# Four model layers on one core: rounding the weights four jobs ahead instead of two

## The chip, the cores and the metric

The kernel runs on one core of a Trainium2 chip in a single launch. TensorE (PE in the profile) multiplies matrices, VectorE (DVE), ScalarE (ACT) and GpSimd (POOL) do elementwise work, and SyncE (SP) issues the transfers of the weights from the chip's memory. Each engine runs its own instructions in the order in which they were written and waits on semaphores for the others. The metric is device time in microseconds (us). The kernel before has a median of 2395.09 us in three runs (2394.77 to 2395.71).

## The reference

256 tokens of 2048 features pass through four residual layers and a last norm, all in float32. Cut to the structure:

```
x = x + cat(chunked_attention(q,k,v) * silu(z_a), glu(gelu(s5(u))) * silu(z_b)) @ w_out   # E1
x = x + forgetting_attention(q,k,v, log_f) * silu(z) @ w_out                              # O1
x = rmsnorm(x)
x = x + cat(hgrn2(q,f,v) * silu(g), nsa(q, six K/V, gates) * silu(g)) @ w_out             # E2
x = x + rglru(conv4(xb)) * silu(g) @ w_out                                                # O2
out = rmsnorm(x)          # q, k, v, u, z, ... are column groups of rmsnorm(x) @ w_in
```

`s5` is a complex state space model of 64 groups, `nsa` sparse attention over 16 heads with compressed keys and values (an MLP on blocks of 32 tokens) and three gates for each head, `rglru` a gated linear recurrence.

## The kernel before, in words

**The stream of weights.** Nearly all of the time goes into the projections. The weights are cut into some 740 *jobs*. A job is two blocks of 128 rows by 512 columns, 512 KB, held as one raw tile of 128x1024. SP loads it (`issue`, the DMA at L281). A float32 product is made of three products of rounded parts: ACT copies the raw tile to a rounded tile `hi` (helper L214), DVE writes the rest `lo` = raw − hi (helper L165), and PE multiplies hi by both parts of the activations and lo by their rounded part (L420). In the W orientation a job is 24 matmuls of 128x256, in the X orientation 12 of 128x512. The activations are split in the same way, once for each group of four feature blocks, into two 4 KB *slots* from a pool of 35 (`Act.split`).

**The loop** (`Kern.run`, L267) emits job by job. At the start of job i, `ahead(i)` calls `prep` for the jobs behind it as long as their width, counted in pieces of 512 columns, stays within `LOOK`; a job counts two. `prep` emits the ACT copy, the DVE subtraction and, if the job's activations are ready, their split. Then come the raw tiles' transfers (`issue(done + RAW)`), the matmuls of job i, and one step of the background. `RAW` is the number of raw tiles, `HL` that of hi and of lo tiles each. So in before the hi and lo of job i+2 are emitted ahead of job i's matmuls, and they need the tiles of job i−2.

**Eleven jobs aren't split**: the forget gate's columns in O1 (one job), the compression weights of E2 (eight, "cmp", in four pairs, L1836 and L219) and its gates (two, "gate", right behind the last pair). PE reads their raw tile itself, so the tile comes free only when their matmuls are done.

**The background** is everything else: attention, S5, HGRN2, NSA, recurrences, norms. Each is a generator, queued in `lane`s. `bg_step` lets each live one do a step after each job, held back by an estimate of how busy DVE, ACT and POOL are, by free PSUM banks and by free slots. If a job's activations are not there yet, the loop forces background steps until they are (`while not all(a.ready ...)`). So the order on every engine comes out of this planning when the program is built, and it changes when `prep` runs earlier: splits and slots are then taken sooner.

**Two places matter below.** At E1's end the gated unit (GLU) multiplies y, the S5's output; y is made block by block, eight blocks, and the second half of the GLU's rows (its first job is number 116) needs the last block (number 7). At E2's end the projection out multiplies the NSA heads' outputs; job 550 needs the last four heads.

Of the kernel before, what the change touches and what calls it, by code (L numbers as in the profile page):

```python
# [11 lines left out]
OP = mybir.AluOpType  # L12
# [14 lines left out]
class Act:  # L27
    """256 columns of tokens for `n` blocks of 128 features, as two float32r parts."""
# [42 lines left out]
class Kern:  # L71
    RAW, HL, LOOK, JK = 5, 4, 4, 2
# [123 lines left out]
    def smax(self, out, a, b, acc):  # L196
        """out = -(a + b); acc = its least, the negative of the greatest of a + b"""
        self._ew('D', self._n(out))
        self.nc.vector.tensor_tensor_reduce(out=out, in0=a, in1=b, op0=OP.add, op1=OP.min,  # L199
                                            scale=-1.0, scalar=3.0e38, accum_out=acc)  # L200
# [26 lines left out]
    def lane(self, gens, width=1, prio=0, name=""):  # L227
        """a queue of (condition, generator maker), `width` of them at a time"""
# [5 lines left out]
    def bg_step(self, force=False):  # L234
# [9 lines left out]
        for L in list(self.lanes):  # L244
            while len(L['live']) < L['width'] and L['q'] and L['q'][0][0]():
                L['live'].append(L['q'].pop(0)[1]())
            for g in list(L['live']):
                if not force and max(self.busy.values()) > self.clock + self.SLACK and L['prio'] > 0:
                    return moved
                # not before what it waits for on another engine is done  # L250
# [3 lines left out]
                try:  # L254
                    r = next(g)
# [11 lines left out]
    def run(self):  # L267
        jobs = self.jobs
        units = []
# [15 lines left out]
        def prep(i):  # L285
            if i >= len(jobs):
                return
            j = jobs[i]
            raw = units[j['u']][1][:, :j['n']]
# [23 lines left out]
        def ahead(i):  # L313
            """the splits of the jobs after job i, as far as LOOK goes"""
# [12 lines left out]
        for i, j in enumerate(jobs):  # L327
            ahead(i)
            # a raw tile is free again once all of it is read
# [29 lines left out]
    def group(self, name, src, acts, orient, post, units, ready=None, bg=False):  # L359
        """one group of 512 columns: `units` is the list of (DRAM AP, kt count)"""  # L360
# [66 lines left out]
def kmap(acts):  # L427
    """k-tile index -> (Act, block in it)"""
    out = []
    for a in acts:  # L430
        out += [(a, i) for i in range(a.n)]
    return out


class Norm:
    """1 / sqrt(mean of squares + eps) for each token, the same on all partitions"""
# [7 lines left out]
    def add(self, src, cols=None):  # L444
        """src: a slot with four blocks of features"""
# [15 lines left out]
    def mean(self, out, extra=None):  # L461
        """generator: out = mean of squares (+ eps), then 1/sqrt"""
# [25 lines left out]
def rsqrt(K, y, v, t):  # L488
    """y = 1 / sqrt(v): a first value by exp(-ln(v) / 2), then a step of Newton"""
# [11 lines left out]
def together(*gens):  # L501
    """the operations of several chains by turns"""
# [9 lines left out]
def steps(n, gen):  # L512
    """n operations at a time"""
# [34 lines left out]
def sincos_ops(K, s, c, x, a, b, d):  # L548
    """sin and cos of x; a, b, d: scratch"""
# [31 lines left out]
    # n mod 4 in -2..2, then a turn by n quarters  # L581
# [10 lines left out]
    K.tt('D', z, z, n, OP.mult)                      # sine of the turn  # L592
    yield
    K.ts('D', r, r, -1.0, 1.0, OP.mult, OP.add)      # cosine of the turn
# [15 lines left out]
def evac_scaled(K, ps, rs, out=None):  # L610
    """a feature-major group times a row of tokens' factors"""
# [13 lines left out]
def evac_silu(K, ps, rs_half, done):  # L625
    """x times sigmoid(x): with h = x / 2 it is (tanh(h) + 1) h"""
# [12 lines left out]
def token_scales(K, rs, out):  # L639
    """generator: factors by token on partitions"""  # L640
# [8 lines left out]
def soft_rows(K, p, nm, sm, cols):  # L649
    """p holds -(s); exp(s - max) with its sums. cols: [(first, end)]"""  # L650
# [4 lines left out]
class E1:  # L655
    """relative-position attention in chunks beside an S5 state space model"""
# [41 lines left out]
    def build(self):  # L698
# [8 lines left out]
        def post_u(i):  # L707
            def f(ps):
                if not self.norm_ok or K.slots.free < 3:
                    return 'wait'  # L710
                # even tokens before odd ones
# [5 lines left out]
                def stack():  # L717
                    """both tokens of a pair on the partitions, for two tiles of states at a time"""
# [66 lines left out]
        def load_bias(hg):  # L785
            def gen():
                [s] = yield from K.gslots(1)
                K.nc.sync.dma_start(s, D['e1_bias'][hg])
                # keys of the chunk after the query's own are out of reach
# [138 lines left out]
        # the first half of y before the second  # L928
# [6 lines left out]
    def s5(self):  # L935
# [30 lines left out]
        def powers():  # L966
            """cosine and sine of 2, 4, .. 128 angles"""
# [9 lines left out]
        def coefs():  # L977
            """A, and the factor of B: (A - 1) / lambda"""
# [20 lines left out]
        def pre():  # L999
# [9 lines left out]
            def times(out, v, re, im, tm):  # L1009
                """a complex number for each state times its coefficients"""  # L1010
# [16 lines left out]
            # cosines and sines of 0, 2, .. 30 times each state's angle  # L1027
# [20 lines left out]
            # y takes the real part: the imaginary parts of C with their sign turned  # L1048
# [7 lines left out]
        def fill(e, pad, src, b):  # L1056
            """block b's coefficients, zero outside of each state's own channels"""
# [11 lines left out]
        def block(b):  # L1069
            def gen():  # L1070
# [7 lines left out]
                # the projections in, the channels of each tile's pairs of tokens on their own rows  # L1078
# [4 lines left out]
                # cosines and sines of 0, 2, .. 254 times each state's angle  # L1083
# [21 lines left out]
                # two tokens a step  # L1105
# [42 lines left out]
                # the even tokens' own inputs: C B  # L1148
# [28 lines left out]
                # gelu by tanh, twice its value  # L1177
# [22 lines left out]
        def yz(i):  # L1200
            def gen():
                # y times silu(z), a quarter of (2 y) (2 silu): y_t is 2 y; sigmoid's half is still to come
# [13 lines left out]
class Layer:  # L1216
    """what the layers share: the norm at their start and the sum with the residual at their end"""
# [15 lines left out]
    def begin(self):  # L1233
        """called when the projection out of the layer before starts"""
# [24 lines left out]
    def take(self, g, ps, xr):  # L1259
        """four blocks of the sum: the residual, and this layer's input"""  # L1260
# [13 lines left out]
def out_proj(K, D, wname, n, acts, xr, nxt, tag):  # L1274
    """xr: list of the residual's slots (filled by the time of use)"""
# [12 lines left out]
def attend(K, S_mm, bias, pv, out, left, done, heads=2):  # L1288
    """generator: two heads at a time, queries on partitions. S_mm(bank, e) emits the scores of head e
    (queries 0..127 with keys 0..127 in columns 0..127, queries 128..255 in columns 128..383)"""  # L1290
# [39 lines left out]
def log1p_ops(K, out, z, s, w, d):  # L1330
    """log(1 + z) for z in 0..1, by the series of atanh(z / (2 + z))"""
# [1074 lines left out]
```

## Time and profile before

| what | value |
|---|---|
| median of the runs | 2395.09 us |
| profiled execution, span | 2394.8 us |
| weight and other data read | 396.00 MB |
| PE busy | 98% of the span |
| DVE busy | 66% |
| ACT busy | 48% |
| DMA engines busy, mean | 51% (queue 1 50.7%) |

The profiled execution's own time is known only as its span; what lies around it is the 0.3 us between span and median. PE's share says that the kernel is a stream of matmuls with few gaps. How the gaps end is told by the waits of PE (which engine and line released it, the total, how often, the longest), by the timeline, and by the granted clock (PEclk, as a share of full speed).

### The profile page before, as it was taken

The page shows a single profiled execution, that of the slowest core. Times are in us where ns is not written, and L with a number is a line of the kernel's source. Part 1 is how long each engine was busy: PE and PEld are TensorE (multiplying, and loading weights), DVE is VectorE, ACT ScalarE, POOL GpSimd, SP SyncE. Part 2 cuts the span into 40 slices and gives each one's busy share as a digit, 9 for nine tenths or more (in the row PEclk, how much of TensorE's full clock was granted, in tenths as well). Part 3 has the DMA queues.
Part 4 walks back from the last instruction along what each step waited for, and adds up shares of the span by engine and source line. Part 5 has one row for each costly group of instructions (what it writes and reads, how often), then busy time and mean ns, then how long its engine had stood idle before and what let it go on. Part 6 is the DMA issues. An engine that isn't in the chain of part 4 may idle for free.

```text
span 2394.8 us, 47663 instructions
## 1 busy us (share of the span) xinstructions
PE 2336.9 (98%) x19906; PEld 2253.3 (94%) x19906; DVE 1585.9 (66%) x2409; ACT 1152.5 (48%) x1662; POOL 386.8 (16%) x320
## 2 busy tenths in 40 slices
PE   7999999999999999999999999999999999999997
PEld 7989998999999999989999999899999999999997
DVE  7978878675554545676758574566667446777764
ACT  5354454444444344543445443455555434666643
POOL 1111211010000000123324253101110000111210
PEclk9999999999999999999999999999999999999999
DMA  6544454555545555554544454554444555555453
GB/s 225 191 152 149 142 177 153 175 186 164 193 160 175 174 170 185 169 177 156 170 160 159 162 165 159 192 178 142 142 142 143 195 183 180 165 175 168 161 196 111
DMA packets 116167, 402.23 MB, mean 168 GB/s; under 512 B 14832, under 2 KB 17776, under 8 KB 115952
## 3 DMA queue, kind: packets, MB, share of 16 engines
q1 hardware_dynamic: 115952, 399.19, 50.7%
q8 instruction: 156, 2.56, 0.4%
q14 instruction: 59, 0.48, 0.1%
HBM read 396.00 MB, written 2.10 MB: 166 GB/s over the span
## 4 chain that ended last, share of the span: by engine, by line
PE 84%; DVE 8%; POOL 2%; issue 2%; ACT 2%; DMA 1%; DVEq 0%; SPq 0%; ACTq 0%; POOLq 0%
PE mm L420 75%; PE b L219 6%; DVE lo L165 3%; DVE s L165 2%; POOL s L165 2%; DVE s L194 1%; DVE s L176 1%; PE b L224 1%; PE b L420 1%; ACT s L214 1%; ACT hi L214 1%; DMA raw<-in_e_in 1%; PE b L1836 0%; DVE s L170 0%; DMA s<-in_e_bias 0%
## 5 line engine op out<-in xcount | busy, mean ns | idle before, releaser
L420 PE MATMUL mm<-s,hi 128*128 128x256 f32 x9984 | 1830.5, 285 | 10.4 <-ACT s L214 7.6
L420 PEld LDWEIGHTS mm<-s,hi 128*128 128x128 f32 x9984 | 1563.9, 193 | 18.3 <-ACT s L214 8.0
L420 PE MATMUL mm<-s,lo 128*128 128x256 f32 x4992 | 1418.6, 284 | 24.5 <-DVE lo L165 24.4
L165 DVE TENSOR_TENSOR lo<-raw,hi 128x1024 fp32r<-128x1024 f32 x730 | 934.0, 1294 | 622.2 <-ACT hi L214 620.4
L214 ACT ACTIVATE hi<-raw 128x1024 fp32r<-128x1024 f32 x730 | 756.9, 1054 | 646.1 <-PE mm L420 557.5
L420 PEld LDWEIGHTS mm<-s,lo 128*128 128x128 f32 x4992 | 960.8, 192 | 28.9 <-DVE lo L165 28.8
L165 POOL TENSOR_TENSOR s<-s,s 128x512 f32<-128x512 f32 (+1 forms) x128 | 273.9, 2154 | 1411.4 <-ACT s L214 586.9
L214 ACT ACTIVATE s<-s 128x1024 f32<-128x1024 f32 (+6 forms) x188 | 132.9, 713 | 263.3 <-DVE s L165 137.2
L420 PE MATMUL mm<-hi,s 128*128 128x512 f32 x768 | 244.6, 394 | 0.0
L219 PE MATMUL b<-s,s 128*32 128x32 f32 (+8 forms) x3008 | 175.0, 244 | 4.8 <-POOL s L186 2.1
L420 PEld LDWEIGHTS mm<-hi,s 128*128 128x128 f32 x768 | 145.0, 189 | 30.8 <-ACT s L214 0.3
L219 PEld LDWEIGHTS b<-s,s 128*32 128x32 f32 (+2 forms) x2976 | 148.3, 135 | 23.4 <-POOL s L186 2.5
L420 PE MATMUL mm<-lo,s 128*128 128x512 f32 x384 | 150.5, 392 | 1.6 <-DVE lo L165 1.6
L214 ACT ACTIVATE s<-b 128x384 f32<-128x384 f32 (+6 forms) x135 | 57.2, 462 | 134.9 <-PE b L219 92.7
L165 DVE TENSOR_TENSOR s<-s,s 128x512 f32<-128x512 f32 (+8 forms) x134 | 85.8, 666 | 45.7 <-ACT s L214 44.5
L420 PEld LDWEIGHTS mm<-lo,s 128*128 128x128 f32 x384 | 72.6, 189 | 16.7 <-DVE lo L165 2.4
L176 DVE SCALAR_TENSOR_TENSOR s<-s,s 128x1024 f32<-128x1024 f32 (+3 forms) x76 | 82.6, 1089 | 3.1 <-ACT s L214 2.2
L214 ACT ACT_TABLE_LOAD x44 | 56.5, 1283 | 16.1 <-DVE s L176 14.7
L204 DVE COPY_PREDICATED s<-hmask,b 32x64 f32<-32x64 int32 (+1 forms) x144 | 36.0, 250 | 30.4 <-PE b L219 26.6
L214 ACT ACTIVATE s<-s,nsam 128x15 f32<-128x15 f32 (+2 forms) x96 | 37.6, 394 | 36.0 <-DVE nsam L199 36.0
L170 POOL TENSOR_SCALAR s<-alibi 128x256 f32<-128x256 f32 x16 | 17.8, 1111 | 212.3 <-PE b L219 174.1
L186 POOL MEMSET s<- 128x512 f32 (+7 forms) x65 | 25.8, 410 | 123.3 <-DMA s<-in_e_bias 59.1
(148 smaller groups left out, 966.6 us busy)
## 6 DMA issues: line engine op xcount, KB each, us to landing
raw<-in_e_in SPq DMA_DIRECT2D x336, 512.0 KB, 4.1
raw<-in_o_in SPq DMA_DIRECT2D x208, 512.0 KB, 4.0
raw<-in_e_out SPq DMA_DIRECT2D x80, 512.0 KB, 4.2
raw<-in_o_out SPq DMA_DIRECT2D x72, 512.0 KB, 4.4
raw<-in_e_outa SPq DMA_DIRECT2D x16, 512.0 KB, 3.6
raw<-in_o_rg SPq DMA_DIRECT2D x10, 512.0 KB, 3.7
raw<-in_e_glu SPq DMA_DIRECT2D x8, 512.0 KB, 3.8
raw<-in_e_cmp SPq DMA_DIRECT2D x8, 512.0 KB, 5.1
```

The source lines that it names most:

```text
L165: self._eng(e).tensor_tensor(out, a, b, op=op)
L170: self._eng(e).tensor_scalar(out, a, s1, None, op0=op0)
L176: self.nc.vector.scalar_tensor_tensor(out, a, s, b, op0=op0, op1=op1)
L186: self._eng(e).memset(out, v)
L194: self.nc.vector.tensor_tensor_scan(out, d0, d1, init, op0=OP.mult, op1=OP.add)
L204: self.nc.vector.copy_predicated(out, mask, a)
L214: self.nc.scalar.activation(out, a, func, scale=scale, **kw)
L219: self.nc.tensor.matmul(out, l, r, start=start, stop=stop, skip_group_check=True, **kw)
L224: self.nc.tensor.transpose(out, a, self.ident[:p, :p])
L420: self.nc.tensor.matmul(out, l, r, start=start, stop=stop, skip_group_check=True)
```

## The change

`LOOK` goes from 4 to 8, so that `prep` runs four jobs ahead instead of two. `HL` goes from 4 to 6 and `RAW` from 5 to 4. `prep` first makes sure that the raw tile of its job has been issued. The program's "dynamic DMA scratch" in the on-chip memory is set to 512 bytes per partition in place of the default of 16384; that pays for the tiles, which take 16 KB more of hi and lo and 4 KB less of raw per partition. All else in the diff is comments taken away, so line numbers behind L289 are one higher after.

```
@@ class Kern
-    RAW, HL, LOOK, JK = 5, 4, 4, 2
+    RAW, HL, LOOK, JK = 4, 6, 8, 2
@@ def prep(i)
             j = jobs[i]
+            issue(j['u'] + 1)
             raw = units[j['u']][1][:, :j['n']]
@@ def kernel
-    nc = bacc.Bacc("TRN2", target_bir_lowering=False, num_devices=1)
+    nc = bacc.Bacc("TRN2", target_bir_lowering=False, num_devices=1, dynamic_dma_scratch_size=512)
```

PE's program has the same instructions in the same order outside of two stretches: E1's jobs 0 to about 120, and E2's jobs 534 to 552. On ACT and DVE the splits stand two jobs earlier against the background everywhere.

**E1's end.** On ACT before, hi_4963 is the rounded weight of job 116, s_4008 the gelu chain of the last S5 block, and s_4866 the split of y's second half, which job 116 multiplies:

```order
L214 ACTIVATE s_4008<-s_4008 128x256
L214 ACTIVATE hi_4802<-raw_4590 128x1024
L214 ACTIVATE s_4008<-s_4008 128x256
L214 ACTIVATE hi_4835<-raw_4635 128x1024
L214 ACTIVATE s_4866<-s_3569 128x1024
L214 ACTIVATE hi_4871<-raw_4677 128x1024
L214 ACTIVATE hi_4901<-raw_4709 128x1024
L214 ACTIVATE hi_4933<-raw_4772 128x1024
L214 ACTIVATE hi_4963<-raw_4806 128x1024
```

On ACT after, job 116's weight is hi_4795; behind it come block 6's gelu (s_4244), block 7's states (s_4969), block 7's gelu (s_4366) and then the split s_5034 of y's second half:

```order
L214 ACTIVATE hi_4795<-raw_4639 128x1024
L214 ACTIVATE hi_4832<-raw_4673 128x1024
L214 ACTIVATE hi_4899<-raw_4713 128x1024
L214 ACTIVATE s_4244<-s_4244 128x256
L214 ACTIVATE hi_4934<-raw_4757 128x1024
L214 ACTIVATE s_4244<-s_4244 128x256
L214 ACTIVATE s_4969<-s_1119 64x8x16 x2
L214 ACTIVATE s_4969<-s_105 64x8x16 x2
L214 ACTIVATE s_4366<-s_825 64x8x16 x2
L214 ACTIVATE hi_4978<-raw_4799 128x1024
L214 ACTIVATE s_4366<-s_4366 128x256 x2
L214 ACTIVATE s_5034<-s_3872 128x1024
```

The split of y stood four weight tiles before the tile of the job that uses it, and now stands five behind it. On PE after, all of block 7 (its 32x32 products, and behind them the rest, which needs copies of these) stands between the job before (mm_4905) and job 116 (mm_4801):

```order
L421 MATMUL mm_4905<-s_3323,lo_4754 128x256
L219 MATMUL b_4985<-s_4969,s_4366 32x32 x8
L219 MATMUL b_4985<-s_862,s_4969 128x128
L219 MATMUL b_4985<-s_4523,s_4969 32x128 x4
L219 MATMUL b_4985<-s_4524,s_4969 32x128 x8
L219 MATMUL b_4985<-s_4523,s_4969 32x128 x4
L219 MATMUL b_4985<-s_4523,s_4969 32x127 x4
L219 MATMUL b_4985<-s_4524,s_4969 32x127 x8
L219 MATMUL b_4985<-s_4523,s_4969 32x127 x4
L421 MATMUL mm_4801<-s_5034,hi_4795 128x256
```

The last S5 block moved to the place just in front of the job that needs it.

**E2's end.** On PE before, b_20348 is the last NSA head's output; the job behind it uses the earlier split s_20286, and the split of the last heads (s_20430) is first used 96 matmul rows further on:

```order
L219 MATMUL b_20348<-s_20102,s_16778 128x128
L219 MATMUL b_20348<-s_20102,s_16947 128x128
L420 MATMUL mm_19902<-s_20286,hi_20282 128x256
L420 MATMUL mm_19902<-s_20287,hi_20282 128x256
L420 MATMUL mm_19902<-s_20286,lo_20283 128x256
```

On PE after, b_20481 is the last head's output and s_20501 the split of the last heads:

```order
L219 MATMUL b_20481<-s_20247,s_16785 128x128
L219 MATMUL b_20481<-s_20247,s_16956 128x128
L421 MATMUL mm_19883<-s_20501,hi_20344 128x256
L421 MATMUL mm_19883<-s_20502,hi_20344 128x256
L421 MATMUL mm_19883<-s_20501,lo_20345 128x256
```

The four jobs that lay between the last head and the job that needs it now lie before that head.

## Rows read from the trace of the kernel before

**Rows 1.** The page: busy us, share of the span and instructions of each engine.
```profile
PE 2336.9 (98%) x19906; PEld 2253.3 (94%) x19906; DVE 1585.9 (66%) x2409; ACT 1152.5 (48%) x1662; POOL 386.8 (16%) x320
```

**Rows 2.** PE's waits, whole span: line, releaser, us in total, times, longest.
```profile
PE mm L420 <- DVE lo L165: 26.0, 21, 2.6
PE mm L420 <- ACT s L214: 7.6, 2, 7.3
PE b L224 <- POOL s L182: 2.2, 1, 2.2
PE b L219 <- POOL s L186: 2.1, 1, 2.1
```

**Rows 3.** PE's waits in 0:120, 360:420, 900:1080 and 2040:2340 us.
```profile
PE mm L420 <- DVE lo L165: 5.9, 3, 2.6
...
PE mm L420 <- DVE lo L165: 3.2, 3, 1.4
...
PE mm L420 <- DVE lo L165: 5.0, 5, 1.1
...
PE mm L420 <- DVE lo L165: 11.9, 10, 2.0
```

**Rows 4.** The chain that ended last: start, us, engine, line, matmuls.
```profile
1831.41 169.91 PE mm L420 x1416
```

**Rows 5.** Timeline in O2: start, us, engine, line, operation, shapes, [idle before, releaser].
```profile
2074.70 4.37 POOL L165 TENSOR_TENSOR s<-s,s 128x1024 f32<-128x1024 f32 x1 [10.88 <-DVE s L194]
2075.73 0.39 PE L420 MATMUL mm<-s,lo 128*128 128x256 f32 x1 [1.48 <-DVE lo L165]
```

**Rows 6.** PE alone behind the longest wait: window, us, busy, PEclk, DMA, GB/s.
```profile
2248.00:2254.00 6.00, 5.97 (x37) 0.72 0.58 193
```

**Rows 7.** Windows of E1: us, PE, PEld, DVE, ACT, POOL busy, PEclk.
```profile
0.00:120.00 120.00, 105.56 (x824) 103.76 (x825) 104.58 (x236) 55.16 (x69) 20.82 (x28) 0.99 0.63 208
360.00:420.00 60.00, 55.90 (x564) 53.99 (x563) 49.20 (x66) 23.97 (x35) 8.12 (x7) 0.97 0.47 157
```

**Rows 8.** The raw tiles: lo's duration in ns (least, median, greatest); landing.
```profile
L165 DVE TENSOR_TENSOR lo<-raw,hi x730: 1160/1225/3425, 6.8 to 2368.2; 128x1024 fp32r<-128x1024 f32 x183
...
DMA to landing us min/median/max: 2.7/4.1/8.0
```

**Rows 9.** Timeline at E1's end, the last S5 block and y's split.
```profile
401.72 0.28 DVE L165 TENSOR_TENSOR s<-b,s5row 128x128 f32<-128x128 f32 x1
...
403.81 2.26 PE L219 MATMUL b<-s,s 128*128 128x128 f32 x66
...
406.14 0.48 DVE L176 SCALAR_TENSOR_TENSOR s<-s,s5d,b 128x256 f32<-128x256 f32 x1 [0.73 <-PE b L219]
...
406.65 0.42 ACT L214 ACTIVATE s<-s 128x256 f32<-128x256 f32 x1 [4.53 <-DVE s L176]
...
409.19 0.29 DVE L172 TENSOR_SCALAR s<-s 128x256 f32<-128x256 f32 x1
...
409.51 0.43 DVE L165 TENSOR_TENSOR s<-s 128x256 f32<-128x256 f32 x1
...
412.97 1.06 ACT L214 ACTIVATE s<-s 128x1024 fp32r<-128x1024 f32 x1 [1.63 <-DVE s L176]
```

**Rows 10.** Timeline of PE in the last cmp job and the gates.
```profile
1549.66 1.97 PE L1836 MATMUL b<-raw,s 128*60 128x128 f32 x32
1551.45 3.62 PE L219 MATMUL mm<-s,raw 128*64 128x256 f32 x32
```

**Rows 11.** Timeline at E2's end: the last NSA head and its split.
```profile
1831.45 0.38 ACT L214 ACTIVATE s<-b 128x256 f32<-128x256 f32 x1 [2.52 <-PE b L219]
...
1831.92 2.41 POOL L165 TENSOR_TENSOR s<-s,s 128x1024 f32<-128x1024 f32 x1 [28.43 <-ACT s L214]
...
1835.17 1.05 ACT L214 ACTIVATE s<-s 128x1024 fp32r<-128x1024 f32 x1
```

**Rows 12.** The page: DMA queue, kind, packets, MB, share of 16 engines.
```profile
q1 hardware_dynamic: 115952, 399.19, 50.7%
```

## The prediction

> **What bounds the kernel now.** I read the page's busy line first, then PE's waits over the whole span and in stretches, the chain, and last the timeline where the order of the change differs. PE is busy for 2336.9 of 2394.8 us [rows 1]. The chain is made of runs of weight jobs: 1416 matmuls, 59 jobs, in 169.91 us, so 2.88 us a job [rows 4]. The change takes no matmul away, so all it can win lies in the 57.9 us in which PE idles, and in the clock that these cost. 7.3 us of that are PE's first wait for a split [rows 2], which the change doesn't touch; the end of the kernel is a chain without weight jobs. The largest part that it can touch is 26.0 us, 21 waits of a weight job for its lo on DVE [rows 2]. They lie in four stretches: 5.9 us in the first 120 us, 3.2 in 360:420, 5.0 in 900:1080 and 11.9 in 2040:2340 [rows 3].
>
> What such a wait is can be seen in O2: PE waits 1.48 us at 2075.73 for a lo, while beside it POOL works through a product for 4.37 us [rows 5]. DVE has elementwise work of its recurrence queued ahead of the lo, and two jobs of lead don't cover it. A wait has a second price. In the six us behind the longest one (1.98 us, ended 2248.03) PE is busy for 5.97 us at a granted clock of 0.72 [rows 6], between the levels of 2.4 and 1.2 GHz: 0.28 × 6 = 1.7 us are lost after PE had idled.
>
> **The change part by part.**
>
> (a) *lo waits behind 900 us.* PE's order is the same there, and lo stands two jobs earlier against the background. The lead grows by 2 × 2.88 = 5.76 us, more than the longest wait and than two waits in a row (at most 4.0). So the 5.0 + 11.9 = 16.9 us go, and with them the 1.7 us of clock behind the longest: 18.6 in full. I take −17.0, since some waits could return elsewhere. If DVE's queue, not its lead, were the limit, about half would stay: bounds −8 and −18.6.
>
> (b) *E1's first 120 us.* 5.9 us of lo waits could go too [rows 3]. But DVE is busy there for 104.58 of 120 us [rows 7], and two more lo stand at the stream's front ahead of everything else: 2 × 1.225 = 2.5 us [rows 8]. I take −3.5; bounds −7 (all waits and some clock) and +3 (the two lo add, nothing goes).
>
> (c) *E1 from 120 to 360 us.* The order is another one here. Two waits for POOL of 2.2 and 2.1 us [rows 2], each with a clock loss as in [rows 6], cost 2.2 + 2.1 + 2 × 1.7 = 7.7 us now. The new order may drop these or have others like them. I take −2, nearer to nothing; bounds −7.7 and +7.7.
>
> (d) *E1's end.* PE now has the last S5 block in a piece between two weight jobs, and job 116, which needs y, right behind. Before, six jobs or more covered the way from y to its split. Nothing covers it now. Between the 32x32 products and the rest of the block (2.26 us for all 66 matmuls), PE waits for copies and a sum: steps of 0.42 and 0.28 us, and on the same two engines one weight tile's hi, 1.06, and lo, 1.23, for hi_4978 is queued there: about 2.7 us with the hand-overs, since part of it overlaps. Behind it come 0.48, 0.42, 0.29, 0.43, another 0.42 and 0.43, and the split's 1.06 and 1.23, in all 4.76 us, and seven hand-overs of about 0.06: 5.2 us [rows 8, 9]. PE idles 7.9 us in two pieces; with 2 × 1.7 us of clock that is 11.3. Now 360:420 has 60 − 55.90 = 4.1 us of idle and 0.03 × 60 = 1.8 us of clock [rows 7], of which 3.2 us are lo waits [rows 3]: 5.9 us that don't come on top. The net is +5.4; bounds 0 (only the second piece is left, and it replaces what is lost now) and +9.5 (the new chain measures like the old way, from y at 403.81 + 2.26 = 406.07 to the end of lo at 412.97 + 1.06 + 1.23 = 415.26, 9.2 us).
>
> (e) *Raw tiles.* With four tiles and preparation four jobs ahead, a split job's tile comes free after landing, hi and lo: 4.1 + 1.06 + 1.23 = 6.4 us, a quarter of it is 1.6 us a job, and with the slowest landing of 8.0 us 2.6 [rows 8, 9], both under 2.88. So the supply holds. Only behind a job that isn't split must the tile wait for PE. For three cmp pairs the jobs beside them (two of 2.75 us in the X orientation) cover the landing. For cmp, cmp, gate, gate PE has work from 1549.66 to 1551.45 + 3.62 = 1555.07 us [rows 10], 5.4 us, and one short product of the gates behind it (I put 0.5). The raw tile asked for goes off when the first of the two cmp jobs is read, half of 1.97 us in; 1.0 + 4.1 + 1.06 + 1.23 makes 7.4 us, against 5.9 of work: a stall of 1.5 us. Bounds 0 and 5.4 (the slowest landing, 8.0).
>
> (f) *E2's end.* The last NSA head's products now stand directly ahead of job 550, which needs the split of that head's output; four jobs stood between. Uncovered are 0.38 (ACT), 2.41 (POOL's product), 1.05 (ACT) and the lo of 1.225 us [rows 8, 11], with hand-overs 5.2 us, and 1.7 us of clock: +6.9. Bounds 5.2 (no clock loss) and 8.9 (POOL's product takes 4.37 us, as in [rows 5]).
>
> This last bound is where a page speaks up. The Trainium skill, "GPSIMD Engine Reference", section Specifications, says that GpSimd shares its SBUF interfaces with VectorE, with contention when DVE reads two SBUF inputs, as a lo does. The trace agrees in one place: 4.37 us beside two lo [rows 5], 2.41 us elsewhere [rows 11]. By the rule the sum would be 2.0 us higher if a lo ran beside; I don't expect it, for while PE stands no weight tile comes free, and the six prepared ones are done.
>
> (g) *Scratch.* All data move on one hardware queue [rows 12], and no queue of the page is one that GpSimd fills. I take 0; if some small transfer did use it, I see no row that could give it a price, and put the bound at ±1 us.
>
> The sum: −17.0 − 3.5 − 2.0 + 5.4 + 1.5 + 6.9 = −8.7 us. 2394.8 − 8.7 = 2386.1 us of span; with the 0.3 us between the span and the median of the runs, 2386.4.
>
> **Rivals.**
>
> *It is faster still: the two stalls don't come.* DVE and ACT, running four jobs ahead, could have done E1's and E2's background so early that the chains of (d) and (f) are shorter, or (c) wins its full 7.7 us. For it speaks that the sums of (d) and (f) are built from rows of another order. Against it, PE's order is fixed: the product of a head and the job that needs it are neighbours in (f), and 4 us of elementwise work can't be done before that product. Without (d) and (f): 2386.4 − 5.4 − 6.9 = 2374; about 2368 to 2380.
>
> *Nothing changes: the waits move.* The same DVE work is there; earlier lo push back the background, whose results PE then awaits. It would win half of (a), −8 in place of −17, beside the other terms' +8.3 (−3.5 − 2.0 + 5.4 + 1.5 + 6.9): 2395.1 − 8.0 + 8.3 = 2395.4. For it speaks DVE's 104.58 of 120 us in E1; against it DVE's 66% over the span, and that in O2 the lo waits come in bursts at a recurrence's scan, not all the time.
>
> *It is slower: E1's blocks run in lockstep.* In E1 slots taken earlier by splits hold up the S5 generators, and these then come to PE one right behind the other, with no job between to cover DVE, ACT or POOL. Each such meeting costs about 2.1 + 1.7 = 3.8 us [rows 2, 6]. The sum of −8.7 is used up by 2.3 meetings beside the one of (d), and 3.6 make the kernel slower by 0.2%. PE's new order shows such neighbours at block 7 alone for certain; in jobs 0 to 116 the blocks have other spacings than before. With five: 2394.8 − 8.7 + 19 = 2405.
>
> *It doesn't do what it says*: raw tiles fail to arrive in time. That is (e); against it is 1.6 us a tile against 2.88 a job.
>
> **How the numbers follow.** The forecast's own range is 2380 to 2391, chance 0.44. Faster still 0.18, no change 0.22, slower 0.16 (0.02 of it for the raw tiles). A measurement of this kernel can tell about 0.2%, 4.8 us, from no change: faster is under 2390.3, slower over 2399.9. So faster 0.44 + 0.18 = 0.62, same 0.22, slower 0.16. The range reaches from 2371, most of the faster case, to 2400, all of the no-change case; what it leaves out is the slower case's upper part and a little of the fastest.
>
> **What would show it.** (a) is right if PE's waits for lo from 900 us on fall from 16.9 us to under 3, wrong if other waits of DVE take their place. (b) and (c): PE's busy time in the windows up to 360 us. (d): a wait of job 116 for its split of some 5 us and one inside the block ahead of it. (f): a wait of a weight job of about 5 us near 1830 us for ACT or DVE, and a PEclk under 0.8 behind it. (e): a wait for hi behind the gates, near 1550. (g): nothing new on the DMA queues. The prediction is wrong if E1's first 420 us grow by more than 8 us, or if the waits of (d) and (f) aren't there.

## The result, and the profile after

The changed kernel takes 2420.83 us (median of four runs, 2418.26 to 2422.5) against 2394.93 us: it is slower, by a ratio of 1.0107 (95% interval 1.0093 to 1.0122). The forecast was 2386.4 us.

The page of the changed kernel, engines, answers to [rows 1]:

```profile
PE 2344.6 (97%) x19906; PEld 2261.5 (93%) x19906; DVE 1578.0 (65%) x2409; ACT 1152.5 (48%) x1662; POOL 382.4 (16%) x320
```

The span grew by 2419.4 − 2394.8 = 24.6 us. PE's idle time went from 57.9 to 2419.4 − 2344.6 = 74.8 us, 16.9 more. The other 7.7 us are PE's busy time, 2344.6 − 2336.9: the same 19906 matmuls ran longer, at a granted clock that over the span is 0.988 in place of 0.995.

PE's waits after, whole span, answer to [rows 2] (line, releaser, us in total, times, longest):

```profile
PE mm L421 <- ACT s L214: 16.0, 4, 7.8
PE mm L421 <- DVE lo L165: 10.4, 9, 2.0
PE b L219 <- ACT s L214: 9.2, 3, 7.2
PE b L219 <- DVE e1m L199: 5.9, 1, 5.9
PE b L219 <- POOL s L186: 4.6, 1, 4.6
PE b L224 <- DVE e1m L199: 3.3, 1, 3.3
PE b L219 <- DVE s L165: 2.6, 2, 2.5
PE b L224 <- DVE s L165: 2.5, 1, 2.5
```

The waits for lo did fall, from 26.0 to 10.4 us. In their place stand a few long waits that before had not: 7.2, 5.9, 4.6, 4.0, 3.8 and 3.3 us. Four of these six are waits of background products (`b`), not of weight jobs.

Where the time changed is read best by stretch. PE's weight jobs stand in the same order in every kernel here, so the first matmul of a given job can be timed in each profile. The table gives, for each stretch of jobs (the unsplit ones not counted), what the stretch takes more or less than in before, in us. Its columns end at the job named; "start" is the first matmul of job 0. Job 104 starts at 391.7 us of before, 118 at 434.9, 440 at 1443.2, 476 at 1569.0, 534 at 1785.7, 552 at 1848.5, 620 at 2045.0 and 700 at 2291.7; from there to the last weight job no kernel differs.

| kernel | start | E1 to 34 | E1 to 104 | E1's end, 118 | to 440 | cmp, gates, 476 | to 534 | E2's end, 552 | to 620 | O2, 700 | sum |
|---|---|---|---|---|---|---|---|---|---|---|---|
| after | +0.5 | −8.7 | +8.1 | +16.6 | −6.7 | +7.9 | −0.8 | +12.1 | 0.0 | −4.4 | +24.6 |
| all_but_look | +0.7 | +0.3 | 0.0 | 0.0 | 0.0 | +2.3 | 0.0 | −0.2 | 0.0 | +1.7 | +4.7 |
| ord4r5 | +0.2 | −0.4 | −1.5 | 0.0 | 0.0 | 0.0 | 0.0 | −0.5 | 0.0 | 0.0 | −2.2 |
| frozen | +7.9 | −5.2 | +0.8 | 0.0 | −6.8 | +9.9 | 0.0 | −0.6 | 0.0 | −4.0 | +1.9 |
| frozen_g | +7.7 | −5.2 | −1.5 | +0.1 | −6.8 | +10.4 | 0.0 | −0.7 | 0.0 | −4.6 | −0.6 |
| split2 | +7.5 | −9.5 | +4.5 | +17.2 | −6.8 | +8.1 | 0.0 | −0.5 | 0.0 | −4.6 | +15.9 |
| raw5 | +0.4 | −8.8 | +5.6 | +17.1 | −6.6 | −0.9 | −0.8 | +10.6 | 0.0 | −10.0 | +6.6 |
| r5split2 | +8.1 | −9.6 | +6.4 | +16.5 | −6.6 | −0.9 | 0.0 | +0.2 | 0.0 | −10.0 | +4.0 |
| r5acct | +0.2 | −2.0 | −4.4 | +2.6 | −6.7 | −0.9 | −0.8 | +11.1 | 0.0 | −10.0 | −11.0 |
| ord8r5 | +0.6 | −4.1 | +1.1 | +0.1 | −6.7 | +0.5 | 0.0 | +0.6 | 0.0 | −10.0 | −18.0 |
| ord6r6 | +0.2 | −2.5 | −2.4 | +0.1 | −6.7 | 0.0 | 0.0 | +0.7 | 0.0 | −7.1 | −17.8 |
| ord8r5f | +0.3 | −3.5 | +1.2 | +0.1 | −6.6 | +1.4 | 0.0 | +0.6 | 0.0 | −15.3 | −21.8 |
| o2fin | +0.3 | −0.6 | −3.3 | 0.0 | 0.0 | 0.0 | 0.0 | −0.4 | 0.0 | −2.7 | −6.7 |

Each profile is one execution: o2fin, which edits nothing in E1, differs there by up to 3.3 us in one stretch and by 3.6 in all from before, so differences of that size between kernels in E1 show nothing. Behind job 118 the kernels that edit nothing in a stretch agree within 0.5 us.

In the changed kernel three places make the loss: E1, the gates, and E2's end.

**E1's end.** The timeline of the changed kernel, PE and then the engines it waited for, answers to [rows 9]:

```profile
431.96 0.33 PE L219 MATMUL b<-s,s 128*32 128x32 f32 x16 [1.02 <-ACT s L214]
...
434.75 0.58 PE L219 MATMUL b<-s,s 128*128 128x128 f32 x1 [2.45 <-DVE s L165]
...
438.71 0.48 DVE L176 SCALAR_TENSOR_TENSOR s<-s,s5d,b 128x256 f32<-128x256 f32 x1 [4.02 <-PE b L219]
439.22 0.42 ACT L214 ACTIVATE s<-s 128x256 f32<-128x256 f32 x1 [6.33 <-DVE s L176]
439.67 0.29 DVE L172 TENSOR_SCALAR s<-s 128x256 f32<-128x256 f32 x1 [0.48 <-ACT s L214]
440.00 0.42 DVE L165 TENSOR_TENSOR s<-s 128x256 f32<-128x256 f32 x1
...
441.37 1.06 ACT L214 ACTIVATE s<-s 128x1024 fp32r<-128x1024 f32 x1 [0.49 <-DVE s L176]
...
442.48 0.58 PE L421 MATMUL mm<-s,hi 128*128 128x256 f32 x1 [3.85 <-ACT s L214]
```

The chain that the prediction drew is there, link by link: the sum inside the block (2.45 us of idle), and after the block the gelu steps to the split (3.85 us). With 1.02 us ahead of them and 0.68 behind, PE idles 8.0 us. PEclk behind each piece is half of full speed, and over the whole stretch from job 104 to 118 it is 0.91 (window, us, PE busy, PEclk, DMA share, GB/s):

```profile
435.00:438.00 3.00, 3.00 (x50) 0.50 0.52 180
442.60:448.00 5.40, 4.72 (x21) 0.50 0.19 58
...
391.70:451.40 59.70, 51.71 (x518) 0.91 0.42 139
```

The same stretch of before, 391.7 to 434.9, holds 43.20 us of PE's work and no idle time. Of the 16.6 us, 4.5 are work that was only moved behind job 104: the block products of 1.95, 0.33 and 2.26 us, which before stand ahead of it. The loss at E1's end is so 12.1 us. That from job 34 to 104 is 8.1 + 4.5 = 12.6, of which 1.7 are 16 background products that stood ahead of job 34 and now stand behind it; the win up to job 34 is smaller by as much.

**The gates.** The timeline of ACT and PE in the changed kernel, behind the last cmp job, answers to [rows 10]:

```profile
1560.38 3.62 PE L219 MATMUL mm<-s,raw 128*64 128x256 f32 x32
1564.11 1.06 ACT L214 ACTIVATE hi<-raw 128x1024 fp32r<-128x1024 f32 x1 [15.55 <-PE mm L219]
...
1566.72 1.06 ACT L214 ACTIVATE hi<-raw 128x1024 fp32r<-128x1024 f32 x1 [1.55 <-DMA raw<-in_e_in]
...
1569.34 1.05 ACT L214 ACTIVATE hi<-raw 128x1024 fp32r<-128x1024 f32 x1
1570.28 0.76 ACT L214 ACTIVATE s<-b 60x256 f32<-60x256 f32 x2
...
1571.19 1.08 PE L219 MATMUL b<-s 128*128 128x60 f32 x4 [7.19 <-ACT s L214]
```

PE waits 7.19 us for a copy of 0.76 us, of the compression's hidden layer, whose input was there from 1560.5 on. That copy stands on ACT behind three hi of weights, and ACT has idled 15.55 us in front of the first. Its raw tile is one that an unsplit job held until PE had read it: its load goes off at 1559.7, when PE is half through the last cmp product, and lands at 1563.7.

**E2's end.** The timeline of the changed kernel answers to [rows 11]:

```profile
1864.09 0.38 ACT L214 ACTIVATE s<-b 128x256 f32<-128x256 f32 x1 [3.42 <-PE b L219]
1864.56 2.34 POOL L165 TENSOR_TENSOR s<-s,s 128x1024 f32<-128x1024 f32 x1 [28.97 <-ACT s L214]
1866.93 1.06 ACT L214 ACTIVATE s<-s 128x1024 fp32r<-128x1024 f32 x1 [2.46 <-POOL s L165]
...
1868.02 1.23 DVE L165 TENSOR_TENSOR s<-s,s 128x1024 fp32r<-128x1024 f32 x1 [6.09 <-ACT s L214]
...
1868.04 0.47 PE L421 MATMUL mm<-s,hi 128*128 128x256 f32 x1 [3.98 <-ACT s L214]
```

Again the predicted chain. POOL's product took 2.34 us, with DVE idle for 6.09 us beside it, so the contention that the Trainium skill's "GPSIMD Engine Reference" states in its section Specifications did not arise here, as forecast; a second wait of 2.5 us, at 1827, was not foreseen. Of the 12.1 us in this stretch 0.8 are eight small products that stood ahead of job 534 before.

**E1's middle.** The longest wait there begins on SP. The timeline of the changed kernel (SP, POOL, ACT, PE):

```profile
131.86 13.32 SPq L281 DMA_DIRECT2D raw<-in_e_in  x4
145.24 0.42 SPq L789 DMA_DIRECT2D s<-in_e_bias  x1
...
150.23 3.16 POOL L186 MEMSET s<- 64x256 f32 x7 [8.40 <-DMA s<-in_e_bias]
151.03 1.90 ACT L214 ACTIVATE s<-s 64x128 f32<-64x128 f32 x6 [5.35 <-POOL s L186]
...
155.97 0.34 PE L219 MATMUL b<-s,s 128*32 128x32 f32 x9 [5.90 <-DVE e1m L199]
```

The load of the attention's bias stands in SP's queue behind four raw tiles' loads, which take 13.32 us to go off, since each waits for its tile. POOL waits for it before it writes the mask into the same tile (the 64x256 memset). The clears of the S5's buffers stand behind that one on POOL, and ACT's copies of the S5 wait for them. A hi of a weight stands behind these copies, its lo stands on DVE ahead of the softmax's first step (e1m), so that step comes late, and PE waits 5.90 us.

**O2.** PE's waits in 2040:2419 us of the changed kernel, answer to the last of [rows 3]:

```profile
PE mm L421 <- DVE lo L165: 8.3, 7, 2.0
...
PE b L421 <- DVE lo L165: 0.9, 1, 0.9
```

All of these end at 2212 us or later. The time between the end of a job's lo and its first matmul tells why (us):

| job | 618 | 636 | 648 | 654 | 666 | 668 |
|---|---|---|---|---|---|---|
| before | 6.2 | 6.2 | −1.8 | 6.2 | −1.8 | −1.2 |
| after | 11.5 | 6.3 | 4.2 | 3.4 | 1.3 | −1.8 |

Before, the lead swings between 6.2 and −1.8 us in each period of 18 jobs, and PE's waits refill it. After, it starts two jobs higher and loses 5.2 us from job 618 to 636 and 2.9 from there to 654; then the waits are back with the sizes they had.

The pace of the two sides can be read apart where PE has lead left and doesn't wait. From job 636 to 654 the changed kernel's PE takes 51.95 us, and the ends of the same 18 lo on DVE lie 54.80 us apart: 2.9 us of lead are lost in a period. With a fifth raw tile (raw5 below) PE takes 51.84 us and the lo 53.33: 1.5 us. In before both take 54.74, since PE is held to the pace of the lo.

### The profile page after: what moved, and what is told of

Same layout as the page of the kernel before. It is cut to its first block, busy times and chain, and to the rows that moved or that the text cites. A ratio compares the mean times of both kernels' runs of the same rounds, so it can differ in the third digit from the quotient of the medians.

```text
span 2419.4 us, 47647 instructions
## 1 busy us (share of the span) xinstructions
PE 2344.6 (97%) x19906; PEld 2261.5 (93%) x19906; DVE 1578.0 (65%) x2409; ACT 1152.5 (48%) x1662; POOL 382.4 (16%) x320
## 4 chain that ended last, share of the span: by engine, by line
PE 76%; DVE 12%; issue 5%; ACT 4%; DMA 2%; POOL 2%; DVEq 0%; SPq 0%; ACTq 0%; POOLq 0%
PE mm L421 68%; PE b L219 6%; DVE lo L165 4%; DVE s L165 4%; ACT hi L214 2%; DVE s L176 2%; ACT s L214 1%; POOL s L165 1%; DVE s L194 1%; PE b L224 1%; DMA raw<-in_e_in 1%; DMA raw<-in_o_in 1%; PE b L421 0%; PE b L1837 0%; ACT L214 0%
## 5 line engine op out<-in xcount | busy, mean ns | idle before, releaser
L421 PEld LDWEIGHTS mm<-s,hi 128*128 128x128 f32 x9984 | 1569.8, 193 | 28.4 <-ACT s L214 16.6
L421 PE MATMUL mm<-s,lo 128*128 128x256 f32 x4992 | 1419.9, 284 | 10.4 <-DVE lo L165 10.4
L421 PEld LDWEIGHTS mm<-s,lo 128*128 128x128 f32 x4992 | 964.0, 193 | 12.6 <-DVE lo L165 12.4
L214 ACT ACT_TABLE_LOAD x44 | 56.5, 1283 | 15.9 <-DVE s L176 14.5
L186 POOL MEMSET s<- 128x512 f32 (+8 forms) x65 | 25.7, 408 | 142.1 <-DVE s L165 73.8
```

The costliest lines, as they stand in the source:

```text
L186: self._eng(e).memset(out, v)
L214: self.nc.scalar.activation(out, a, func, scale=scale, **kw)
L421: self.nc.tensor.matmul(out, l, r, start=start, stop=stop, skip_group_check=True)
```

## The experiments

Twelve kernels. The code shown is cut, and `...` marks what is left out. The ratio is to the kernel before, with its 95% interval.

**all_but_look.** Everything of the change but the deeper lead.
```
-    RAW, HL, LOOK, JK = 4, 6, 8, 2
+    RAW, HL, LOOK, JK = 4, 6, 4, 2
```


> LOOK stays at 4 (two jobs ahead); four raw tiles, six hi and lo tiles and the scratch of 512 bytes are in. Theory A (the time is lost by what LOOK moves: the order in E1 and at E2's end, and ACT's queue at the unsplit jobs): 2395 us, within 3 of before. Rival B (the storage costs: four raw tiles are too few, or the small scratch slows transfers): 2405 to 2420 us.


Measured: 2398.95 us, ratio 1.0019 (1.0010 to 1.0028). The storage costs 2.3 us at the gates and 1.7 in O2 even with a lead of two jobs. So it has a price, small as long as the lead is two jobs.

**ord4r5.** The scratch and the early issue alone.
```
-    RAW, HL, LOOK, JK = 4, 6, 8, 2
+    RAW, HL, LOOK, JK = 5, 4, 4, 2
```


> The kernel before with the small scratch and the early issue alone (five raw tiles, four hi and lo tiles, two jobs ahead). Theory A (the 4.6 us that all_but_look lost come from the fourth raw tile): 2394.5 us within 1.5. Rival (the scratch or the issue costs): 2398 to 2400 us.


Measured: 2394.62 us, ratio 0.9998 (0.9989 to 1.0006). Scratch and issue are free within the interval. What all_but_look lost is so put down to the fourth raw tile in place of a fifth; the two kernels also differ by two hi and two lo tiles, which were not tried alone.

**frozen.** hi and lo four jobs ahead; the planner's account and the activations' splits two ahead.
```
+                kept, last = dict(self.busy), self.last
...
+                self.busy, self.last = kept, last
...
+        def near(i):
...
+            j = jobs[i]
+            if j['split']:
+                self._cost('A', 200 + j['n'] * 0.84)
+                self._ew('D', j['n'])
...
             for a in j['acts']:
                 if a.ready:
                     a.split()
```


> hi and lo are prepared four jobs ahead as in the changed kernel, but the planner accounts for them, and splits activations, two jobs ahead as before, so that PE's order is the one of before. Theory A: E1's and E2's end lose their new waits, the wait behind the gates stays (+8.8 us), lo waits shrink by about 6.7 us at 900 to 1460, 5 in O2 and 8 in E1: 2395 + 8.8 - 20 = about 2384 us, and between 2378 and 2390. Rival B (the longer lead itself does harm, by hi and lo standing ahead of the background on ACT and DVE): 2405 us or more.


Measured: 2398.42 us, ratio 1.0016 (1.0007 to 1.0025). The new waits of E1 and E2's end are gone, as theory A has it, but the time is its 2384 us plus 14. The start, which it left out, costs 7.9 us, because in this kernel the first activations' split stands on ACT behind four hi. E1 behind the start wins 4.4 of the 8 us forecast and O2 4.0 of 5. The gates cost 9.9 us, near the 8.8 forecast, but not by the wait forecast. PE waits there for the gate's own raw tile, which DVE scales and which now stands behind the lo of weights further ahead (PE's waits in 1500:1640 us of frozen):

```profile
PE mm L219 <- DVE raw L165: 7.9, 1, 7.9
```

**frozen_g.** frozen, with no job prepared more than two ahead while an unsplit job lies between.
```
+                if w > 4 and not all(jobs[m]['split'] for m in range(max(i, 0), k + 1)):
+                    break
```


> As frozen, but no job is prepared more than two ahead while a job that isn't split lies between. Theory A: the wait behind the gates (8.8 us) goes too, so 8 to 9 us less than frozen, about 2376 us. Rival (that wait comes from having four raw tiles in place of five, whatever stands in ACT's queue): the same time as frozen within 3 us.


Measured: 2397.31 us, ratio 1.0008 (0.9999 to 1.0017). The gates still cost 10.4 us, so the time is the rival's. The waits are again others: the longest are one of 3.5 us for a lo and one of 1.8 for the copy. That the number of raw tiles is behind all of them is shown by raw5, not by this kernel.

**split2.** The changed kernel with the splits alone two jobs ahead (`presplit` does what the lines taken away did, for the next two jobs).
```
-            for a in j['acts']:
-                if a.ready:
-                    a.split()
...
             ahead(i)
+            presplit(i)
```


> The changed kernel, but activations are split two jobs ahead as before; the planner still accounts for the weights four jobs ahead. PE's order is that of the changed kernel in E1 and that of before at E2's end. Theory A (at E2's end the early splits take the slots that the last head needs): the 11.8 us at jobs 534 to 551 go, 2421 - 12 = 2409 us. Rival (E2's end is lost to the tiles of weights standing in ACT's and DVE's queues, not to slots): 2418 us or more.


Measured: 2412.86 us, ratio 1.0078 (1.0064 to 1.0092). E2's end falls from +12.1 to −0.5, so the early splits make that loss, as theory A said; that they do it by the slots which they take is not shown. The start costs 7.5 us as in frozen, which the expectation left out. E1's end stays at +17.2.

**raw5.** The changed kernel with a fifth raw tile.
```
-    RAW, HL, LOOK, JK = 4, 6, 8, 2
+    RAW, HL, LOOK, JK = 5, 6, 8, 2
...
-    nc = bacc.Bacc("TRN2", target_bir_lowering=False, num_devices=1, dynamic_dma_scratch_size=512)
+    nc = bacc.Bacc("TRN2", target_bir_lowering=False, num_devices=1, dynamic_dma_scratch_size=64)
```


> The changed kernel with five raw tiles (paid by a scratch of 64 bytes); PE's order is that of the changed kernel. Theory A (at the gates the copies of the unsplit jobs' results stand on ACT behind hi of weights whose raw tiles can't be loaded yet): one more tile lets one more hi through, so PE's wait of 7.2 us at the gates falls by about a job, 2.9 us, and the time to about 2417 us; E1's and E2's end stay. Rival (the number of raw tiles doesn't matter there): 2421 us within 2.


Measured: 2403.34 us, ratio 1.0037 (1.0023 to 1.0050). The gates' wait goes altogether. ACT and PE there:

```profile
1546.69 1.06 ACT L214 ACTIVATE hi<-raw 128x1024 fp32r<-128x1024 f32 x1 [5.49 <-DMA raw<-in_e_in]
...
1552.71 1.06 ACT L214 ACTIVATE hi<-raw 128x1024 fp32r<-128x1024 f32 x1 [4.96 <-DMA raw<-in_e_in]
...
1558.64 1.06 ACT L214 ACTIVATE hi<-raw 128x1024 fp32r<-128x1024 f32 x1 [0.33 <-DMA raw<-in_e_in]
1559.60 0.75 ACT L214 ACTIVATE s<-b 60x256 f32<-60x256 f32 x2
...
1561.71 0.66 PE L219 MATMUL b<-s 128*128 128x60 f32 x4
```

The same three hi stand ahead of the copy on ACT. But the first two ran at 1546.69 and 1552.71, before PE's last cmp product at 1556.36, and ACT idles only 0.33 us in front of the third. The lead in O2 also lasts longer (−10.0 for −4.4), since the lo come faster there, as told under O2. Theory A had the cause, but "about a job" was too little and O2 was left out. The scratch of 64 bytes was not tried alone; ord6r6, with more than four raw tiles and 512 bytes, loses nothing at the gates either.

**r5split2.** raw5's and split2's edits together.


> The changed kernel with five raw tiles and the activations' splits two jobs ahead; the planner still accounts for the weights four jobs ahead. Theory A (the gates' wait, E2's end and E1 are three separate causes that add up): 2403.3 - 12 (E2's end) + 7 (start, as split2 has it) = about 2398 us, with E1 as in the changed kernel. Rival (they share a cause): above 2402 or under 2394 us.


Measured: 2399.29 us, ratio 1.0015 (1.0006 to 1.0023). The causes add up, as theory A said: the gates −0.9, E2's end +0.2, the start +8.1, and E1 about as in the changed kernel.

**r5acct.** raw5 with frozen's account two jobs ahead; the splits stay four ahead, in `prep`.
```
+            if j['split']:
+                self._cost('A', 200 + j['n'] * 0.84)
+                self._ew('D', j['n'])
```


> The changed kernel with five raw tiles and the planner's account two jobs ahead as before; activations are split four jobs ahead. Theory A (E1 loses its 16 us by the early account, E2's end its 12 us by the early splits): E1's part goes, E2's end stays, 2403.3 - 14 = about 2389 us. Rival (the early splits upset E1 as well): 2398 us or more.


Measured: 2386.08 us, ratio 0.9957 (0.9945 to 0.9970). E1 from the start to job 118 goes from raw5's +0.4 − 8.8 + 5.6 + 17.1 = +14.3 to −3.6 us; E2's end stays at +11.1. So the early account makes E1's loss, and the early splits make E2's, as theory A said.

**ord8r5.** frozen_g with five raw tiles, and at each step the next two jobs before those further ahead.
```
+            for lim in (4, self.LOOK):     # first two ahead with their splits, then the rest
```


> As frozen_g, with five raw tiles, and at each step the next two jobs' weights and splits are emitted before the weights further ahead, which puts the first split back in front of the third weight. Theory A: the start's 7.7 us go and most of the 6 to 8 us at the unsplit jobs, so 2397 - 13 = about 2384 us; lo waits stay in the second half of O2. Rival (the lead itself costs what it gives): 2393 us or more.


Measured: 2378.54 us, ratio 0.9929 (0.9916 to 0.9941). It beats both kernels by more than either theory gave: the deeper lead, with before's order and before's five raw tiles, is worth 17 us.

**ord6r6.** The same, three jobs ahead.
```
-    RAW, HL, LOOK, JK = 5, 6, 8, 2
+    RAW, HL, LOOK, JK = 6, 5, 6, 2
```


> As ord8r5, but three jobs ahead in place of four (six raw tiles, five hi and lo tiles). Theory A (in O2 the elementwise loop takes longer than PE, so a deeper lead is a stock that is used up once): one job less of stock, O2 gives back about half of its 10 us, 2378.5 + 4 to 5 = about 2383 us, and its lo waits begin about one period of 55 us earlier. Rival (a lead longer than the longest wait hides them all, at three jobs as at four): 2377 to 2380 us.


Measured: 2379.41 us, ratio 0.9932 (0.9918 to 0.9945). The time is the rival's. O2 goes theory A's way but by less: it wins 7.1 us in place of ord8r5's 10.0, 2.9 given back for 4 to 5 expected, and its waits for lo begin at 2124 us in place of 2233, about two periods earlier and not one. E1 from the start to job 118 is at −4.6 in place of −2.3, a difference within what two profiles differ by there.

**o2fin.** The kernel before, one product of O2 on DVE.
```
-                K.tt('G', ht[i], ht[i], st['g', i], OP.mult)
+                K.tt('D', ht[i], ht[i], st['g', i], OP.mult)
```


> The kernel before with one edit in O2: the product of the recurrence's result and its gate (five of them) moves from GpSimd to VectorE. PE's order stays. Theory A (the lo waits in O2 come from ACT: the split of that product waits there 7.4 us for GpSimd, and four hi of weights wait behind it): the ten waits of 11.9 us go, and with them some clock, 2394.5 - 13 = about 2381 us. Rival (VectorE has too much to do there): it gets 1.2 us more for each product, 2394 us or more.


Measured: 2393.26 us, ratio 0.9988 (0.9979 to 0.9997). The time is near the rival's, and theory A was wrong in the main: nine waits of 10.2 us stay in O2 in place of ten of 11.9, and O2 wins 2.7 us in place of 13. A wait of about 1.46 us stays in every period; the other is of 0.7 us, where before had one of 0.9 and once one of 2.0. So moving POOL's product takes away little of what makes these waits. The move also adds about 1.2 us of work to DVE each time, and the two effects were not told apart.

**ord8r5f.** ord8r5 with o2fin's edit.


> As ord8r5, with o2fin's product on VectorE. Theory A: half of the loop's excess goes, so the lead lasts to the end of O2; the one wait left there (1.98 us and its clock) goes, 2378.5 - 3 = about 2375 us. Rival (VectorE's own load empties the lead): 2380 us or more.


Measured: 2375.03 us, ratio 0.9911 (0.9897 to 0.9924), the best kernel of the study. PE's waits in 2040:2373 us:

```profile
PE b L219 <- ACT s L214: 1.0, 1, 1.0
PE mm L436 <- DVE lo L165: 0.7, 1, 0.7
```

The stock now lasts to the end of O2, as theory A said: from job 618 to 690 the 72 lo take 214.3 us in place of ord8r5's 219.8. The edit is worth 2.7 us in O2 on its own, 5.3 here.

## Why the prediction was wrong

The forecast was −8.7 us and the profile shows +24.6, 33.3 apart. By its own steps:

- **(a), behind 900 us:** forecast −17.0, measured −6.7 − 4.4 = −11.1. To job 440 it won 6.7 us, more than the 5.0 of waits. In O2 it won 4.4 of about 12. The step that failed is that the lead, once longer than two waits in a row, makes the waits go. That holds for a burst. In O2 the lo come slower than PE uses them, 54.80 us against 51.95 for 18 jobs, so the lead is a stock that is drained; ord6r6 and ord8r5f move it as a stock does. The bound of −8 had named this case, but the value was taken at the other end. The fourth raw tile has a large part in it, which (e) with its "So the supply holds" left out: with a fifth (raw5) the drain from job 636 on is half as fast and O2 wins 10.0, which with 6.6 to job 440 is nearly the forecast. Price: 5.9 us.
- **(b) and (c), E1 ahead of its end:** forecast −3.5 − 2.0, and with the 5.9 us of before's losses in 360:420, which (d) took off though they lie ahead of job 104, −11.4. Measured from the start to job 104, with the moved work put back: +0.5 − 8.7 + 8.1 + 4.5 = +4.4. The front's lo waits fell from 5.9 to 2.1 us; then come waits of 5.9, 3.3 and 4.6 us where before had 2.2 and 2.1. This is like the rival of blocks meeting at PE, but the cause which that rival gave, slots taken early by splits, is not it: with the splits back at two jobs (split2) the loss stays, and with the splits early and the account back (r5acct) it goes. "The new order may drop these or have others like them" was the step that failed: the order was known there, and its new neighbours were not walked through as in (d) and (f). raw5 against r5acct shows the cause, `prep` booking hi and lo into the planner's account two jobs sooner, by which background is emitted later. 15.8 us.
- **(d), E1's end:** 7.9 us of idle and 3.4 of clock forecast, 11.3 together; 8.0 and about 4 measured, 12.1 together. The place and the chain were right; that the sum fits so well is in part luck. The piece inside the block measured 2.45 us for 2.7 forecast, the one behind it 3.85 + 0.68 = 4.53 for 5.2, and a third, of 1.02 us ahead of the block, was not forecast. Its net of +5.4 was wrong by the 5.9 us told under (c). 0.8 us.
- **(e), the gates:** forecast +1.5, measured +7.9. The step that failed is the queue: I followed the raw tile to the job that multiplies it, and not to what stands behind its hi on ACT. A copy that PE needed at once was there. It takes both the lead and the tiles: with four raw tiles the gates lose 2.3 us at a lead of two jobs (all_but_look) and 7.9 at four; with five they lose 0.0 (ord4r5) and win 0.9 (raw5). 6.4 us.
- **(f), E2's end:** forecast +6.9, measured +12.1. The place and the chain were right: PE idles 3.98 + 0.79 = 4.8 us there for 5.2 forecast. A second wait of 2.5 us wasn't foreseen, the clock behind the two cost more than the 1.7 priced, and 0.8 us are the work that moved past job 534. The early splits are the cause (split2, r5split2). The bound with POOL's 4.37 us rested on a wrong reading of [rows 11], told in the last section; it didn't enter the sum. 5.2 us.
- **(g), scratch:** 0 was right (ord4r5).
- **The clock** was priced at 1.7 us for each wait, from a wait of 1.98 us, which the prediction calls the longest; it is the longest behind 900 us, and [rows 2] has one of 2.6. Behind longer ones it costs more: after the 4.60 us wait PEclk is 0.50 over the whole of a 5.5 us window, where before's window behind 2.08 us shows 0.60 over 3.5 us. After and before:

```profile
346.50:352.00 5.50, 5.50 (x40) 0.50 0.27 95
```

```profile
136.00:139.50 3.50, 3.50 (x25) 0.60 0.22 47
```

That is 2.75 us against 1.4 lost in these windows alone. Over the kernel PE's busy time grew by 7.7 us.

These differences add up: 5.9 + 15.8 + 0.8 + 6.4 + 5.2, less the 0.8 that the stretch to job 534 is shorter, make the 33.3 us. The two stalls that the forecast read out of the new order, (d) and (f), came where it put them. The sign was wrong by E1's middle, the gates and O2: 15.8 + 6.4 + 5.9 = 28.1 of the 33.3 us.

What stays open: how the planner's earlier account makes E1's three middle waits in detail. The bias load behind raw tiles on SP is seen in the trace, but was not tried alone. Open too is what sets the pace of the lo in O2 beside the number of raw tiles; moving POOL's product (o2fin) changed it little.

## What to carry to other kernels

A deeper prefetch is worth its depth once, unless the engines that fill it are faster than the one that drains it over the whole stretch: compare their times per period (here 53 to 55 us against 52) before counting the waits as gone. When a prefetch is issued earlier on an in-order engine, ask what stands behind it there; a copy that waits for its tile holds up everything behind it, and one more buffer for the tile (the fifth raw tile, 17 us) can matter more than the depth. If a planner orders the rest, give it the old account and the old moments for what isn't prefetched: the same four-job lead cost 25.9 us with the order moved and won 17 us with the order kept and a fifth raw tile.

## What the hardware showed beside this

POOL's 128x1024 product took 2.34 us with DVE idle, 2.41 us at [rows 11] and 4.37 at [rows 5] beside two lo. The prediction took the 2.41 us for a product with no lo beside it. But a lo did run beside it, from 1832.82 on (DVE's timeline of before, there and at [rows 5]):

```profile
1832.82 3.72 DVE L165 TENSOR_TENSOR lo<-raw,hi 128x1024 fp32r<-128x1024 f32 x2 [2.44 <-ACT hi L214]
...
2074.47 2.34 DVE L165 TENSOR_TENSOR lo<-raw,hi 128x1024 fp32r<-128x1024 f32 x2
```

At 1832.82 POOL had begun first and kept its time, and two lo took 3.72 us. At 2074.47 DVE began first: its two lo took 2.34 us, and POOL's product, begun at 2074.70, was the one that got longer. So in these two places the engine that began later paid. That a lo beside the product makes it 2.0 us longer, as the prediction has it under (f), holds only where the lo begins first.

The price of a wait in clock isn't the same for each: windows behind waits of 2.08 and 4.60 us lost 1.4 and 2.75 us.
